# Key pages into the recurrent branch, later stores, a shorter weight lead: one edit to the order of work in a decoder layer

## The chip, the cores and the metric

The kernel runs on one core of a Trainium2 chip. The core has a matrix engine (TensorE, PE in the profile, with its weight loads as PEld), a vector engine (VectorE, DVE), an activation engine (ScalarE, ACT), a general engine (GpSimd, POOL) and a sync engine (SyncE, SP). In this kernel nearly every transfer between device memory and the on-chip buffer is issued from SP, in one order; sixteen DMA engines carry them out. Each engine runs its instructions in the order in which they were placed, and waits at an instruction until its operands and its buffer are there. The metric is the device time of one execution in microseconds (us), as the median of a few runs.

## The reference: one layer of a hybrid decoder

A prompt of 512 tokens and 8 sample sequences of one token each go through one layer with the same weights; the kernel treats them as 520 columns. Model width is 1024, there are 16 heads of 64.

```python
sh1, sc1, g1, sh2, sc2, g2 = ada_modulation(c, ada_w, ada_b)
h = rms_norm(x, norm1_g) * (1 + sc1) + sh1
xr, gr, q, k, v, fl, ga, gb = split(h @ w_in)
# branch A: recurrent
xc = causal_conv4(xr);  hr = rg_lru(xc)          # gates, exp, linear scan over time
ya = (hr * gelu(gr)) @ w_proj_a
# branch B: attention with a forget gate
logf = log_sigmoid(fl + b_f);  F = cumsum(logf)
s = q.k / 8 + F[t] - F[s]                         # prompt: causal, 512 x 512 per head
yb = (softmax(s) @ v) @ w_proj_b                  # samples: 1024 cached tokens and their own
# merge and feed-forward
x = x + g1 * ((sigmoid(ga) * ya + sigmoid(gb) * yb) @ w_o)
x = x + g2 * swiglu(rms_norm(x) * (1 + sc2) + sh2)
```

The samples' cached keys and values lie in pages of 128 tokens (128 x 1024 floats, 512 KB). Each of the 8 sequences has 8 key pages and 8 value pages, found through a page table. Outputs are the layer's result, k, v and logf of all tokens, and the states of the convolution and of the recurrence.

## The kernel before: units of work, and page work hung between them

**Units.** All large products are cut into units of 128 output columns: a product of the 1024 x 128 weight tile with the 1024 x 520 activations. For precision both are split into a high and a low part, so that a unit is 48 matmuls in two halves of 260 columns (`half_product`, line 231). The units have one fixed order. Units 0 and 1 are the last two of q; 2 to 31 are the recurrent branch (xr, gr, ga, gb of eight tiles i, in four stages of two tiles; the first stage is units 2 to 7, the others have eight each); 32 to 41 are k of tile 0, the eight units of the projection `pa`, and v of tile 0; 42 to 55 are k and v of tiles 1 to 7 inside the attention loop; 56 and 57 are the last two gb units; then come `pb`, `w_o` and the feed-forward part.

**Weights ahead.** `begin` opens a unit. It issues the loads of later weights (`load_chunks`, two buffers `wraw` of 1 MB) up to a reach of 22 us of estimated unit time, and splits weights (`split_upto`: ACT makes `whi`, DVE makes `wlo`, lines 197 and 198; three buffers each) up to a reach of 11 us. One unit counts 0.67 x 8 = 5.4 us in that estimate, so the reaches are four units and two units.

**Pages between units.** The samples' attention over the cache is done in small steps between units:

- `key_page` loads a key page (line 587) into one of seven buffers `pg` and multiplies it on POOL with the sequence's query `qb` (line 603); `qb` takes one of the seven buffers for eight pages.
- `key_sums` then reduces the page on DVE (line 614), a number of ticks after the load. 16 key pages (two sequences) make one group r.
- `past_softmax` is the softmax chain of a group, in five steps over successive ticks (lines 640 to 670), across DVE, PE, ACT and DMA.
- `sample_values` multiplies a pair of value pages with the weights of a group (line 687, matmuls on PE). Eight pairs make a group; `value_pages` keeps one pair loaded ahead.

`tick(keys, values)` does these in the order sums, chain steps, value pairs, key pages. It is called from `begin` for units 4 to 41, where the tables `KEYS` and `VALUES` tell how many key pages and whether a value pair; and from `at(i, part)` four times in each iteration i of the attention loop, by `KEYS_AT` and `VALUES_AT`. In `begin` the key pages come last, behind the weight loads. A step can only be taken when the one before it has been: a value pair of a group is skipped while the group's chain isn't done.

**The recurrent branch.** Per tile: convolution (`conv`, DVE lines 798 and 800, with the gate weights `gws`), two gate products (`lru_gates`), exponentials on ACT and line 829 on DVE (`lru_exp`), the scan over time on DVE (`lru_scan`, lines 840 to 843), and the product with the gelu (`lru_mul`, `lru_g`).

**The forget chain.** `log_forget` (lines 545 to 561) loads the logits, forms log sigmoid on ACT and DVE in small instructions, stores it, loads it back as 16 rows, fills a tile `fone` of ones on POOL (line 559), scans with it on DVE (line 560) and stores the sums `ftd` (line 561). It is called in the first stage, behind the second convolution.

**The attention loop.** Iteration i has the unit of k of tile i+1 and of v of tile i+1 (in the last iteration the two gb units), and around them for tile i: the transposes of v (`v_tokens`), the transposes of the probabilities (`turn`), scores and softmax of the next tile (`scores`), and the product with the values (`values`). `q_load` and `decay_rows` load q and the forget sums `fb` of a tile; `fm` (line 999) is made of `fb` on POOL.

**Stores.** `gate_b`, `branch_a`, `k_product` and `v_product` each end with a store of their result (lines 870, 879, 952, 975), issued right behind the unit.

**Who sets the order.** A list scheduler places the instructions of each engine when the kernel is built. It follows the order of the text as a priority and puts an instruction later where it takes its operands to be late. `issue_after` pins an instruction behind another on its engine; a key sum is pinned behind the last split (`state["last"]`).

## Time and profile before

| what | us |
|---|---|
| median of 3 runs | 1132.02 |
| lowest and highest of them | 1130.69, 1138.16 |
| the profiled execution's own time | 1130.33 |
| its span, first to last instruction | 1128.6 |
| PE busy in the span | 1052.2 |
| DVE, ACT, POOL busy | 654.1, 496.8, 295.7 |
| data moved | 206.95 MB |

All durations come from the one profiled execution. Its own time is 1.7 us above its span, and 1.7 us below the median of the runs. A busy time is the union of an engine's instructions; a busy PE isn't always a PE at full rate, since its clock can be granted below full speed (row `PEclk`, in tenths) and a matmul that waits inside its queue counts as busy.

Along the span, by the profile: norm, first modulation and q up to about 105 us; the recurrent branch from there to 313; `pa` to 381; the attention loop from 381 to 625; `pb` and `w_o` to about 725; the feed-forward part to the end.

### The profile page before, as it was taken

Reading aid. Unit: us, or ns where it says so; the run is one execution under the profiler, and the core shown is the slowest. Engines: PE = TensorE matmul, PEld = TensorE weight load, DVE = VectorE, ACT = ScalarE, POOL = GpSimd, SP = SyncE. Lnnn points to the kernel's source line nnn. Section 1 sums busy time; section 2 is a strip of 40 time slices with the busy share of each in tenths; the row PEclk is TensorE's granted clock in tenths of the full one; section 3 lists DMA queues with packets and bytes.
Section 4 is the critical chain, followed back from the end, with each engine's and each line's share of the span. In section 5 each row is a group of like instructions: output and inputs, shape, how many; then the busy total and the mean of one; then the engine's idle time right before and its main releaser. Section 6 shows DMA issues by size and latency. Waiting matters only on the chain.

```text
span 1128.6 us, 21038 instructions
## 1 busy us (share of the span) xinstructions
PE 1052.2 (93%) x8210; PEld 959.4 (85%) x8210; DVE 654.1 (58%) x1265; ACT 496.8 (44%) x983; POOL 295.7 (26%) x262
## 2 busy tenths in 40 slices
PE   4999969999998988878899899999999999999996
PEld 2877969999987856656678798999999999999995
DVE  6445897777775767967665454763334333443355
ACT  4424545777722555545567223453321233212352
POOL 2202571214244667757330001410000000000013
PEclk9999989999999998889899899999999999999998
DMA  9795655566689799998886485222323333242312
GB/s 336 266 346 175 211 189 163 177 209 172 212 287 295 192 318 300 292 284 291 246 229 241 150 292 179 75 76 76 113 75 105 83 89 99 79 109 76 94 57 76
DMA packets 164982, 206.95 MB, mean 183 GB/s; under 512 B 9475, under 2 KB 125715, under 8 KB 164819
## 3 DMA queue, kind: packets, MB, share of 16 engines
q1 hardware_dynamic: 164802, 205.09, 57.4%
q8 instruction: 64, 1.05, 0.4%
q0 software_dynamic: 80, 0.52, 0.2%
q14 instruction: 36, 0.29, 0.1%
HBM read 192.49 MB, written 13.09 MB: 182 GB/s over the span
## 4 chain that ended last, share of the span: by engine, by line
PE 67%; DVE 9%; DMA 5%; ACT 3%; issue 1%; POOL 1%; SPq 0%; DVEq 0%; POOLq 0%; ACTq 0%
PE fo L231 11%; PE fiu L231 10%; PE fig L231 10%; PE pb L231 4%; PE pa L231 4%; PE v L231 3%; PE pv L687 3%; PE ga L231 3%; PE wo L231 2%; PE k L231 2%; PE gb L231 2%; PE gr L231 2%; DVE wlo L198 2%; PE po L1073 1%; DMA pg<-in_cache_v_dram 1%
## 5 line engine op out<-in xcount | busy, mean ns | idle before, releaser
L198 DVE TENSOR_TENSOR wlo<-wraw,whi 128x1024 fp32r<-128x1024 f32 (+1 forms) x131 | 166.2, 1269 | 151.9 <-ACT whi L197 151.6
L197 ACT CAST whi<-wraw 128x1024 fp32r<-128x1024 f32 (+1 forms) x131 | 136.5, 1042 | 224.2 <-PE fo L231 74.6
L603 POOL TENSOR_TENSOR pg<-pg,qb 128x1024 f32<-128x1024 f32 x64 | 164.9, 2589 | 131.6 <-DMA pg<-in_cache_k_dram 109.3
L306 POOL TENSOR_TENSOR ss<-ss,sq 128x260 f32<-128x260 f32 x18 | 13.6, 755 | 424.8 <-ACT sq L305 424.4
L614 DVE TENSOR_REDUCE S<-pg 128x16 f32<-128x1024 f32 x64 | 77.1, 1211 | 40.2 <-POOL pg L603 40.2
L231 PE MATMUL fiu<-h2h,whi 128*128 128x260 f32 x320 | 90.5, 283 | 0.0
L231 PE MATMUL fig<-h2h,whi 128*128 128x260 f32 x320 | 90.4, 283 | 0.0
L231 PE MATMUL fiu<-h2l,whi 128*128 128x260 f32 x320 | 90.4, 283 | 0.0
L231 PE MATMUL fig<-h2l,whi 128*128 128x260 f32 x320 | 90.4, 283 | 0.0
L231 PE MATMUL fiu<-h2h,wlo 128*128 128x260 f32 x320 | 90.3, 282 | 0.0
L231 PE MATMUL fig<-h2h,wlo 128*128 128x260 f32 x320 | 90.3, 282 | 0.0
L231 PE MATMUL fo<-ach,whi 128*128 128x260 f32 x292 | 82.6, 283 | 0.0
L231 PE MATMUL fo<-acl,whi 128*128 128x260 f32 x292 | 82.5, 283 | 0.0
L231 PE MATMUL fo<-ach,wlo 128*128 128x260 f32 x292 | 82.5, 283 | 0.0
L687 PE MATMUL pv<-pg,pw 128*32 128x512 f32 x256 | 53.3, 668 | 15.6 <-DMA pg<-in_cache_v_dram 11.4
L231 PEld LDWEIGHTS fiu<-h2h,whi 128*128 128x128 f32 x320 | 60.2, 188 | 0.0
L231 PEld LDWEIGHTS fig<-h2h,whi 128*128 128x128 f32 x320 | 60.2, 188 | 0.0
L231 PEld LDWEIGHTS fig<-h2h,wlo 128*128 128x128 f32 x320 | 60.2, 188 | 0.0
L231 PEld LDWEIGHTS fiu<-h2h,wlo 128*128 128x128 f32 x320 | 60.2, 188 | 0.0
L231 PEld LDWEIGHTS fiu<-h2l,whi 128*128 128x128 f32 x320 | 60.2, 188 | 0.0
L231 PEld LDWEIGHTS fig<-h2l,whi 128*128 128x128 f32 x320 | 60.2, 188 | 0.0
L1024 ACT ACTIVATE p<-p,mu 128x128 f32<-128x128 f32 (+3 forms) x64 | 35.5, 556 | 47.7 <-DVE mu L1022 47.5
(373 smaller groups left out, 3452.6 us busy)
## 6 DMA issues: line engine op xcount, KB each, us to landing
pg<-in_cache_k_dram SPq DMA_DIRECT2D x64, 512.0 KB, 5.8
pg<-in_cache_v_dram SPq DMA_DIRECT2D x64, 512.0 KB, 6.2
araw<-in_ada_w_dram SPq DMA_DIRECT2D x48, 512.0 KB, 7.4
wraw<-in_w_fi_dram SPq DMA_DIRECT2D x44, 512.0 KB, 5.2
wraw<-in_w_in_dram SPq DMA_DIRECT2D x34, 512.0 KB, 6.2
wraw<-in_w_in_dram SPq DMA_DIRECT2D x11, 1024.0 KB, 5.7
wraw<-in_w_fo_dram SPq DMA_DIRECT2D x8, 1024.0 KB, 5.2
x<-in_xT_dram SPq DMA_DIRECT2D x16, 260.0 KB, 6.1
```

Source lines behind the costliest of these rows:

```text
L197: state["act"] = act.copy(hi[:, :k1 - k0], src)
L198: state["last"] = dve.tensor_tensor(lo[:, :k1 - k0], src, hi[:, :k1 - k0].bitcast(F32), ALU.subtract)
L231: pe.matmul(out[:, :HALF], lhsT=wt[k], rhs=at, start=k == 0 and m == 0, stop=k == nk - 1 and m == 2)
L306: eng.tensor_tensor(acc[:, t0:t1], acc[:, t0:t1], q_, ALU.add)
L603: pool.tensor_tensor(pg, pg, qb[0], ALU.mult)
L614: dve.tensor_reduce(S[r // 2][:, c:c + H], pg.rearrange("p (h d) -> p h d", d=DH), AX.X, ALU.add)
L687: pe.matmul(pv[0][32 * gq:32 * gq + 32, :], lhsT=pw[r][:, c:c + 32], rhs=pgs[gq // 2][:, 512 * hf:512 * hf + 512], start=j == 0, stop=j == ...
L1024: act.activation(p[:, :n + 128], p[:, :n + 128], AF.Exp, bias=mu[:, 1:2], scale=-1.0, accum_out=mu[:, 2:3])
L1073: pe.matmul(po[:, 128 * kb:], lhsT=kvs[i]["v"][kb // 2][:, kb % 2, 128 * a:128 * a + 128], rhs=pair[m][:, o_:o_ + n], start=kb == 0 and m ...
```

## The change: where pages, stores, splits and the forget chain are put

The page work, the arithmetic and the units stay the same. What is moved:

- **Key pages.** `KEYS` now gives 48 pages to units 4 to 41 where it gave 38: 36 to units 4 to 31 (24 before) and 12 to units 32 to 41 (14 before). `KEYS_AT` gives 16 to the attention loop (26 before), one per part in iterations 0 to 3; before it was six in each of these and two in iteration 4. In `begin` the key pages now come ahead of the weight loads and of the sums, and in `tick` behind the load of a value pair.
- **Value pairs.** `VALUES` has 11 units from 21 on (8 before, from 26 on). `VALUES_AT` has three and two pairs in turn, where it had three in each iteration.
- **Stores.** Four kinds of stores (sB, tA, kT, vT) are put into a list and issued by `flush`, at the end of the next `begin` or `at`.
- **Weights in attention.** The reaches are set to 14 us (two units) for loads and 8 us (one unit) for splits from the start of the attention loop until the end of iteration 6, and back to 22 and 11 then.
- **Forget chain.** `log_forget` is called at the end of the second stage, not in the first. Its scan multiplies with a broadcast of a column of ones in place of the tile `fone`, so the fill on POOL goes.

```diff
-    state = {"n": 0, "dma": 0, "split": 0}
+    state = {"n": 0, "dma": 0, "split": 0, "load": 22, "lead": 11}
+    stores = []
+
+    def store(dst, src):
+        stores.append((dst, src))
+
+    def flush():
+        while stores:
+            sp.dma_start(*stores.pop(0))
+
-    KEYS = {4: 2, 5: 2, 6: 2, 7: 2, 12: 2, 13: 1, 14: 2, 15: 1, 20: 2, 21: 1, 22: 2, 23: 1, 28: 1, 29: 1, 30: 1, 31: 1,
-            32: 1, 33: 2, 34: 1, 35: 2, 36: 1, 37: 2, 38: 1, 39: 2, 40: 1, 41: 1}
-    VALUES = range(26, 42, 2)
+    KEYS = dict(zip(range(4, 42), (2, 2, 2, 2, 0, 1, 0, 1, 2, 2, 2, 2, 0, 1, 0, 1, 2, 2, 2, 2, 0, 1, 0, 1, 1, 2, 1, 2,
+                                   1, 1, 1, 1, 2, 1, 1, 2, 1, 1)))
+    VALUES = range(21, 42, 2)
...
-        load_chunks(units[reach(n, last, 22)][0])
-        split_upto(reach(n, last, 11))
-        if 4 <= n < 42:
-            tick(KEYS.get(n, 0), n in VALUES)
+        paced = 4 <= n < 42
+        if paced:
+            key_pages(KEYS[n])
+        load_chunks(units[reach(n, last, state["load"])][0])
+        split_upto(reach(n, last, state["lead"]))
+        if paced:
+            tick(0, n in VALUES)
+        flush()
...
-        fone = slot("fone", NP, parts=H)
-        pool.memset(fone, 1.0)
-        dve.tensor_tensor_scan(fcs, fone, lf[:, :NP], 0.0, ALU.mult, ALU.add)
+        dve.tensor_tensor_scan(fcs, one_col[:H].to_broadcast([H, NP]), lf[:, :NP], 0.0, ALU.mult, ALU.add)
...
+    def key_pages(n):
+        for _ in range(n):
+            if keys_todo:
+                key_page(*keys_todo.pop(0))
...
         some_values(values)
-        for _ in range(keys):
-            if keys_todo:
-                key_page(*keys_todo.pop(0))
         value_pages()
+        key_pages(keys)
...
-        sp.dma_start(sBd[i], t)
+        store(sBd[i], t)
...
-        sp.dma_start(tAd[i], tA[i])
+        store(tAd[i], tA[i])
...
-            log_forget()
...
             both(lru_exp, i)
+            if i == 2:
+                log_forget()
...
-        sp.dma_start(kT[128 * i:128 * i + 128, :], t)
+        store(kT[128 * i:128 * i + 128, :], t)
...
-        sp.dma_start(vT[128 * i:128 * i + 128, :], t)
+        store(vT[128 * i:128 * i + 128, :], t)
...
-    KEYS_AT = [(2, 1, 2, 1)] * 4 + [(2, 0, 0, 0)] + [(0, 0, 0, 0)] * 3
-    VALUES_AT = [(1, 1, 0, 1)] * 7 + [(1, 2, 1, 0)]
+    KEYS_AT = [(1, 1, 1, 1)] * 4 + [(0, 0, 0, 0)] * 4
+    state.update(load=14, lead=8)
+    VALUES_AT = [(1, 1, 0, 1), (1, 0, 0, 1)] * 3 + [(1, 1, 0, 1), (1, 1, 1, 1)]
 
     def at(i, part):
         tick(KEYS_AT[i][part], VALUES_AT[i][part], 2)
+        flush()
...
         if i == KT - 2:
             merge_load(0)
+            state.update(load=22, lead=11)
 
     def join():
+        assert not values_todo and not chains
```

## The prediction, made before the result was known

> **What bounds the kernel now.** I read the page's first two parts, then cut the attention loop and the branch into stretches, then read who waits for whom, last the instructions in order of time.
>
> ```profile
> span 1128.6 us, 21038 instructions
> PE 1052.2 (93%) x8210; PEld 959.4 (85%) x8210; DVE 654.1 (58%) x1265; ACT 496.8 (44%) x983; POOL 295.7 (26%) x262
> ...
> PEclk9999989999999998889899899999999999999998
> DMA  9795655566689799998886485222323333242312
> ```
>
> PE is busy for 93% of the span, so only its 76 us of idle time and its slowed clock can be won. The DMA row has a plateau of 8 and 9 in slices 14 to 21, and 5 and 6 in slices 4 to 10: the engines that bring pages are full in attention and half empty in the branch. The next view gives busy time per engine for the attention loop's first seven of eight iterations (cut where the k unit starts) and for `pa`; the last three columns are the granted clock, the DMA share and the rate.
>
> ```profile
> 381.20:414.90 33.70, 27.45 (x182) 20.91 (x182) 22.96 (x53) 16.67 (x42) 22.49 (x12) 0.95 0.89 253
> 414.90:446.60 31.70, 27.49 (x177) 20.94 (x176) 23.93 (x63) 18.75 (x47) 27.01 (x19) 0.89 0.91 302
> 446.60:479.40 32.80, 29.17 (x183) 22.74 (x182) 30.46 (x75) 18.27 (x48) 24.12 (x17) 0.90 0.97 292
> 479.40:513.90 34.50, 27.81 (x178) 21.09 (x179) 21.96 (x59) 18.17 (x47) 22.35 (x16) 0.90 0.86 258
> 513.90:544.80 30.90, 27.11 (x177) 21.27 (x177) 22.01 (x65) 17.33 (x45) 18.12 (x13) 0.89 0.92 302
> 544.80:576.30 31.50, 26.78 (x185) 20.86 (x183) 20.32 (x65) 19.11 (x50) 9.62 (x11) 0.95 0.85 226
> 576.30:601.60 25.30, 25.30 (x188) 19.93 (x189) 14.86 (x53) 18.18 (x47) 7.47 (x7) 1.00 0.88 307
> ...
> 313.00:381.20 68.20, 62.92 (x465) 55.38 (x466) 44.14 (x82) 19.45 (x38) 31.27 (x18) 0.97 0.89 289
> ```
>
> Iteration 6 is the yardstick: PE busy throughout, at full clock, 25.3 us. Iterations 0 to 4, in which key pages run, take 163.6 us together, 32.7 each, at clocks of 0.89 to 0.95 and a DMA share of 0.86 to 0.97. Iteration 5 has no key page and still takes 31.5. The waits of the attention loop (total us, times, longest):
>
> ```profile
> PE pv L687 <- DMA pg<-in_cache_v_dram: 11.4, 7, 3.7
> PE pv L687 <- ACT pw L658: 4.1, 1, 4.1
> ...
> SPq L975 <- ACT vt L250: 29.5, 6, 6.8
> SPq L870 <- ACT sB L869: 10.5, 1, 10.5
> SPq L879 <- DVE tA L878: 7.8, 1, 7.8
> SPq L952 <- ACT kt L944: 4.2, 4, 3.0
> ```
>
> PE's largest wait is for value pages. SP stands 52.0 us at the four kinds of stores, because each is issued before its result exists, and every page load behind it stands too.
>
> In the recurrent branch, by stage:
>
> ```profile
> 120.60:170.20 49.60, 39.83 (x316) 39.23 (x316) 48.38 (x35) 24.18 (x41) 34.49 (x16) 0.90 0.55 187
> 170.20:217.90 47.70, 47.36 (x396) 47.15 (x394) 33.99 (x45) 31.90 (x58) 11.00 (x8) 1.00 0.54 172
> 217.90:262.00 44.10, 44.10 (x362) 43.51 (x363) 33.48 (x48) 33.70 (x58) 7.89 (x7) 1.00 0.55 173
> 262.00:313.00 51.00, 50.87 (x416) 46.75 (x415) 38.86 (x49) 36.48 (x65) 20.07 (x7) 1.00 0.65 202
> ```
>
> PE is the bound in the last three; in the first, DVE is busy 98% and PE idles 9.8 us. Why DVE is full there:
>
> ```profile
> PE gr L231 <- DVE wlo L198: 8.0, 2, 7.7
> ...
> 120.65 8.11 DVE L560 TENSOR_TENSOR_SCAN fcs<-fone,lf 16x512 f32<-16x512 f32 x1 [4.24 <-POOL fone L559]
> ...
> 158.47 2.31 DVE L800 SCALAR_TENSOR_TENSOR xc<-prm,xc 128x8 f32<-128x8 f32 x1
> 166.87 0.21 DVE L800 SCALAR_TENSOR_TENSOR xc<-prm,xc 128x8 f32<-128x8 f32 x1
> ...
> 120.10 0.52 POOL L559 MEMSET fone<- 16x512 f32 x1
> 120.58 7.10 POOL L603 TENSOR_TENSOR pg<-pg,qb 128x1024 f32<-128x1024 f32 x3
> ...
> SPq L561 <- DVE fcs L560: 14.6, 1, 14.6
> SPq L587 <- DVE S L614: 16.4, 10, 5.2
> ```
>
> The scan of the forget chain first waits 4.24 us for the fill with ones on POOL, then takes 8.11 us beside three page products. It isn't alone: the same 128x8 instruction takes 0.21 us or 2.31 us, the long one beside page products. SP stands 14.6 us at the store of the scan's result, with pages and weights behind it.
>
> **The change, part by part.**
>
> *Pages leave attention.* DMA time in iterations 0 to 4 is share times length: 30.0 + 28.8 + 31.8 + 29.7 + 28.4 = 148.7 us. Rate times length gives 45.9 MB, so 3.24 us per MB, and 1.70 us for a page of 512 KB. Ten key pages go, one of the three query broadcasts (same size), and two value pairs of 15 (3+2+3+2+3 remain), four pages: 15 x 1.70 = 25.5 us. Left are 123.2 us, 24.6 per iteration, just under PE's 25.3. Today an iteration loses (163.6 - 148.7) / 5 = 3.0 us beyond its DMA time. I take the larger limit plus that loss, 28.3: 5 x 28.3 = 141.5, **-22.1 us**. Iteration 5 holds the 4.1 us wait for the last group's softmax; that group's pages now end an iteration earlier, so 28.3 here too, **-3.2 us**. The last two iterations stay. Ends: all six at 25.3, 195.1 - 151.8, gives -43.3; all of 0 to 4 at iteration 5's 31.5 gives -6.1.
>
> Those ten pages also leave POOL and DVE in attention; neither is the bound in iteration 6, so I count nothing for it.
>
> *Stores later.* No instruction is added. The 52.0 us that SP stands go, and value pages start sooner; that is how the 28.3 is reached, so it isn't added again. Each store still has its room behind it. Their tiles live a unit longer in the 60 slots of the heap; I see no row that prices it and count nothing between 0 and one store's wait, 6.8 us.
>
> *Weights less far ahead.* Same loads and splits, later. A unit lasts about 12.6 us in attention (half of 25.3). The row below lands a load in 6.2 us, and the split behind it takes 1.28, so one unit of lead covers both. I take nothing; if the queue delays a load by a whole unit, 6.2 us once per tile is the end, and that is part of the 3.0 kept.
>
> ```profile
> wraw<-in_w_in_dram SPq DMA_DIRECT2D x34, 512.0 KB, 6.2
> ...
> L198 DVE TENSOR_TENSOR wlo<-wraw,whi 128x1024 fp32r<-128x1024 f32 x22 | 28.2, 1280 | 13.8 <-ACT whi L197 13.6
> L614 DVE TENSOR_REDUCE S<-pg 128x16 f32<-128x1024 f32 x15 | 18.0, 1209 | 0.0
> ...
> L829 DVE SCALAR_TENSOR_TENSOR th<-gate,th 128x520 f32<-128x520 f32 x8 | 12.8, 1602 | 5.0 <-ACT gate L828 5.0
> L800 DVE SCALAR_TENSOR_TENSOR xc<-prm,xc 128x8 f32<-128x8 f32 x21 | 10.9, 517 | 0.0
> L842 DVE TENSOR_TENSOR gate<-a,prm 128x8 f32<-128x8 f32 x8 | 6.8, 849 | 8.7 <-ACT a L826 8.7
> ...
> 255.42 0.17 DVE L842 TENSOR_TENSOR gate<-a,prm 128x8 f32<-128x8 f32 x1 [4.20 <-ACT a L826]
> 258.65 0.69 DVE L829 SCALAR_TENSOR_TENSOR th<-gate,th 128x520 f32<-128x520 f32 x1
> ...
> L603 POOL TENSOR_TENSOR pg<-pg,qb 128x1024 f32<-128x1024 f32 x25 | 69.7, 2803 | 94.6 <-DMA pg<-in_cache_k_dram 84.3 <-DMA gw<-in_gates_dram 7.5 <-PE gate L817 2.8
> ```
>
> *Forget chain.* In the built order of the changed kernel the small steps of log sigmoid stay in the first stage; the scan and its store move into the second. The first stage loses 4.24 us of waiting and the scan's 8.11, more than PE's 9.8 us of idle time: **-9 us** (ends 0 and -9.8). The scan with the broadcast operand has no row; it costs between 1.2 us (a scan of that length elsewhere in the branch) and 8.11. I take 4, as page products will run beside it again.
>
> *Pages enter the branch.* Units 8 to 31 get 28 key pages, where 16 were. Each costs a reduction of 1.21 us on DVE, and holds other DVE instructions while its product runs. The hold per page is between 0 and 2.1 (2.31 less 0.21). Three groups show it in the branch: 8 x (1.60 - 0.69) + 21 x (0.52 - 0.21) + 8 x (0.85 - 0.17) = 19.2 us over 25 pages, 0.8 each; with the groups not quoted I take 1.0. So 12 x 2.2 = 26.5 us. The second group's softmax chain moves here from `pa`: I estimate 5 us for its six DVE steps, the longest of which took 2.17 us for the first group. DVE in the last three stages goes from 106.3 to 106.3 + 26.5 + 4 + 5 = 141.8 of 142.8 us: full. The first stage shows what a full DVE costs, 9.8 us in 50. The splits' lead of two units (11.5 us) delays that, and the load isn't even, so I take one such loss and less, **+8 us**, with ends 0 and 3 x 9.8 = 29.4.
>
> ```profile
> 241.33 2.17 DVE L649 TENSOR_SCALAR dg<-cs,st 32x256 f32<-32x256 f32 x1
> ```
>
> *`pa`.* Two key pages fewer, value pairs equal: 3.4 us less DMA time where PE idles 5.3 us: **-1 us**.
>
> The GPSIMD Engine Reference of the Trainium skill (section "8. Key points") says that GpSimd and VectorE contend for SBUF when the vector instruction has two SBUF inputs or a two-port mode. The trace agrees for the 128x8 instruction (2.31 against 0.21 us) and hardly for the two-input split, whose mean is 1.28 against 1.21 for a reduction with one input. What it would make of the time if all of it held is the second rival.
>
> Sum: -22.1 - 3.2 - 9 + 8 - 1 = -27.3 us, from the profiled execution's 1130.3 to **1103 us**. That execution is 1.7 us below the median of the runs.
>
> **The rivals.**
>
> *Attention isn't bound by DMA.* Iteration 5 speaks for it: 31.5 us with no key page at 226 GB/s, so the chain of splits, scores and transposes across engines may set the pace. Iteration 6, with more bytes per us (307) and no loss, speaks against. Then iterations 0 to 4 give only 6.1 us, and with -2 for the rest: 1122 us.
>
> *Every page holds DVE for its whole product.* Twelve more products of 2.37 us (7.10 for three) hold 28.4 us in place of the 12 counted: DVE is over its room in the branch by the 16 us of difference and PE waits for it: 1103 + 16 = 1119 us. For it: the first stage. Against: the groups above, which show 0.8 us a page. This is the rule quoted above, taken at full strength.
>
> *Slower: pages ahead of weights choke SP.* In `begin` the page loads now stand ahead of the weight load. A page load waits for one of seven buffers, which a reduction on a full DVE frees; behind it stand the weights, the gate weights and the stores, and behind these ACT's and DVE's splits and PE. The longest such wait today is 5.2 us. I count twelve units of stages two to four, the ones that take two pages or load weights behind one; from 27.3 / 12 = 2.3 us lost at each the kernel is slower. At two thirds of 5.2 us, 3.5 each, 42 us are lost: 1103 + 42 = 1145 us. Against it: the reach of four units is 23 us, and a load lands in 6.2.
>
> *The change doesn't do what it says*: value pairs are skipped because a group's chain is late, and pages fall back into attention. The tables give 16 pages by unit 14 and the first pair at unit 21, seven ticks later for five steps, so this is unlikely: 1130 us.
>
> *More than forecast*: iterations at 25.3 and no loss in the branch, -43.3 - 9 = -52: 1078 us.
>
> **How the numbers follow.** Forecast 0.52, attention bound elsewhere 0.12, full hold 0.11, choked queue 0.12, no effect 0.05, more than forecast 0.08. About 1% is what a measurement here can tell from no change: 1119 to 1141 counts as same when put against 1130.3. Faster gets the forecast, the better case, and something under half of the two rivals at 1122 and 1119: 0.69. Same gets the rest of these and no effect: 0.19. Slower is the choked queue: 0.12. The range leaves out most of the better case and the choked queue, and reaches from 1086 to 1130.
>
> **What would show it.** Right: iterations 0 to 4 near 28 us with a PE clock above 0.95 and a DMA share still above 0.9; PE's wait for value pages under 6 us; SP's wait at the four stores gone; no PE idle time of 8 us in the first stage; DVE above 0.9 in stages two to four with few PE gaps. Wrong: iterations still at 31 us with a falling DMA share (bound elsewhere); PE waits for `wlo` in stages two to four above 15 us in all (hold); SP waiting for pages with weights landing late (choke).

## The result, and the profile after

| | before | changed |
|---|---|---|
| median, us | 1132.04 | 1119.75 |
| lowest to highest, 4 runs each | 1130.69 to 1138.16 | 1117.42 to 1121.52 |
| span of the profiled execution | 1128.6 | 1117.0 |

The ratio is 0.988, with a 95% interval of 0.9839 to 0.9921: the kernel is faster by 12.3 us, where 27.3 were forecast. First the page of the changed kernel: span, busy time, granted clock and DMA share in 40 slices.

```profile
span 1117.0 us, 21038 instructions
...
PE 1046.2 (94%) x8210; PEld 960.8 (86%) x8210; DVE 660.9 (59%) x1265; ACT 496.2 (44%) x982; POOL 297.8 (27%) x261
...
PEclk9999989999899989898999999999999999999998
DMA  9795857577779777787985595123324242332312
```

The DMA row is more even now: mostly 5 to 8 where the branch had 5 and 6, and the plateau of 8 and 9 in attention has broken up. So pages did move. The eight iterations of the attention loop of the changed kernel, cut as before (busy time of PE, PEld, DVE, ACT, POOL, then clock, DMA share and rate):

```profile
386.20:424.60 38.40, 30.31 (x183) 22.57 (x182) 23.47 (x51) 13.78 (x34) 15.31 (x12) 0.87 0.59 192
424.60:459.20 34.60, 26.92 (x171) 22.13 (x170) 21.73 (x60) 18.60 (x47) 21.15 (x14) 0.85 0.77 226
459.20:487.00 27.80, 26.25 (x180) 20.14 (x179) 21.27 (x58) 17.99 (x46) 17.58 (x12) 1.00 0.83 278
487.00:518.90 31.90, 25.95 (x169) 22.47 (x168) 24.05 (x65) 18.22 (x46) 22.11 (x14) 0.84 0.76 242
518.90:542.80 23.90, 23.90 (x181) 19.71 (x179) 20.59 (x62) 18.69 (x46) 9.36 (x10) 1.00 0.92 262
542.80:573.00 30.20, 27.46 (x198) 20.80 (x198) 16.97 (x64) 18.33 (x48) 9.01 (x10) 1.00 0.90 275
573.00:595.10 22.10, 22.10 (x177) 19.57 (x176) 15.73 (x54) 18.30 (x48) 7.42 (x7) 1.00 0.90 335
595.10:615.20 20.10, 18.53 (x155) 17.38 (x153) 13.59 (x48) 17.41 (x35) 1.31 (x1) 1.00 0.36 126
```

Iterations 2 and 4 are what was forecast or better. Iterations 0, 1 and 3 are not, and their DMA share is 0.59 to 0.77: it isn't mainly pages that they lack. In each of the three PE is idle for 6 to 8 us **and** runs at a clock of 0.84 to 0.87. The branch of the changed kernel, by stages, the last cut at the beginning of `pa` (in the kernel before, `pa` begins at 310.3 us, 2.7 us ahead of the cut at 313):

```profile
120.60:170.20 49.60, 44.11 (x351) 43.90 (x350) 44.47 (x45) 27.64 (x50) 38.87 (x18) 0.93 0.60 204
170.20:217.90 47.70, 45.93 (x377) 45.07 (x377) 43.51 (x48) 31.13 (x54) 21.83 (x11) 1.00 0.65 195
217.90:262.00 44.10, 44.10 (x363) 41.17 (x363) 34.13 (x40) 26.38 (x48) 19.90 (x9) 1.00 0.83 270
262.00:322.00 60.00, 53.76 (x414) 49.18 (x413) 49.02 (x60) 39.20 (x66) 26.23 (x15) 0.94 0.73 230
```

The second and third stage take their pages nearly without loss, and DVE is far from full in the third. The fourth loses. To see what was lost as what, I split each stretch three ways: PE's idle time; the loss to the clock (busy time times one less the granted clock, summed over stretches of 2 us); and the rest, which is PE's own work. The difference of after to before, in us (the first two rows are the branch, with the first stage's forecast in the first and that of the pages in the second):

| stretch (us, before / after) | all | idle | clock | own work | forecast |
|---|---|---|---|---|---|
| 105 to the end of the last xr unit (269 in both) | 0 | -2.8 | +0.7 | +2.2 | -9 |
| from there to k of tile 0 (35.4 / 45.8) | +10.4 | +6.2 | +3.0 | +1.1 | +8 |
| k of tile 0 and `pa` (76.6 / 71.4) | -5.2 | -3.6 | 0 | -1.6 | -1 |
| attention (243.6 / 229.0) | -14.6 | -5.1 | -2.6 | -6.8 | -25.3 |
| `pb` to the end (504.0 / 501.8) | -2.2 | +0.1 | -3.0 | +0.7 | 0 |

The sum is the 11.6 us of the span. Within attention, iterations 0 to 4 fell by 7.0 (22.1 forecast), iteration 5 by 1.3 (3.2), and 6 and 7 by 6.1 (none forecast). The own work of -6.8 there is mostly value pairs: 24 fewer of their matmuls (three pairs), which keep PE busy for 31.7 us where it was 41.9 (slowed clock included), and 24 in the last two iterations where 48 were. Some of them appear as the +2.2 in the branch.

### Where the fourth stage lost: a small instruction beside a page product

The fourth stage of the changed kernel in stretches of 4 us (same columns), where before PE was busy throughout:

```profile
276.00:280.00 4.00, 4.00 (x36) 4.00 (x36) 2.99 (x7) 2.19 (x5) 0.40 (x3) 1.00 1.05 394
280.00:284.00 4.00, 1.96 (x17) 1.75 (x15) 4.00 (x4) 0.00 (x0) 4.00 (x2) 1.00 0.15 58
284.00:288.00 4.00, 0.74 (x3) 0.74 (x4) 4.00 (x4) 1.70 (x5) 2.19 (x1) 0.81 0.71 187
288.00:292.00 4.00, 4.00 (x21) 4.00 (x20) 4.00 (x5) 3.72 (x7) 0.49 (x1) 0.50 0.99 339
292.00:296.00 4.00, 4.00 (x28) 3.02 (x28) 3.29 (x4) 3.69 (x9) 1.90 (x1) 0.83 0.48 160
```

ACT does nothing from 280 to 284 and PE next to nothing from 282 to 288; then PE runs at half clock for 4 us. The instructions of POOL, DVE and ACT there, in order of time (start, duration, then who ended the idle time):

```profile
279.71 0.22 DVE L814 SCALAR_TENSOR_TENSOR xc<-prm,xc 128x8 f32<-128x8 f32 x1
...
279.92 6.26 POOL L614 TENSOR_TENSOR pg<-pg,qb 128x1024 f32<-128x1024 f32 x2 [2.00 <-DVE xc L814]
...
280.51 2.34 DVE L814 SCALAR_TENSOR_TENSOR xc<-prm,xc 128x8 f32<-128x8 f32 x1
...
283.91 2.30 DVE L814 SCALAR_TENSOR_TENSOR xc<-prm,xc 128x8 f32<-128x8 f32 x1
...
286.30 0.62 ACT L270 CAST xch<-xc 128x520 fp32r<-128x520 f32 x1 [7.03 <-DVE xc L814]
286.83 0.38 ACT L871 ACTIVATE ge<-gr 128x260 f32<-128x260 f32 x1
```

Two page products run from 279.92 us on; both are done after 6.26 us. The 128x8 instruction ahead of them takes 0.22 us, the two beside them 2.34 and 2.30. ACT stands 7.03 us at `xch`, which needs the last of them; behind it on ACT stands `ge`, which empties the buffer that PE's next product needs. The view of PE's waits of this stage has it:

```profile
PE ga L244 <- ACT ge L871: 5.3, 1, 5.3
```

That the products are the cause is shown by the runs without them, below. The clock adds to it: behind 5.3 us of idle time in two stretches PE got half its clock. The Trainium skill has this as a rule (TensorE: Matmul & The Clock Gate, section "Part 1: The HAM clock gate (the "warmup" mystery)"): an idle window of some 3.4 us halves the clock, and a busy one of that length restores it. The trace agrees: 0.50 from 288 to 292 us, behind the gap, and 0.83 in the next stretch, in which the full clock comes back. So 6.2 us of idle time in this stage cost 9.2.

### Where attention lost: the third group's chain at the seam

The changed kernel around the end of `pa` (386.1) in stretches of 4 us: PE busy, clock, DMA share, rate.

```profile
384.00:388.00 4.00, 4.00 (x35) 1.00 0.05 18
388.00:392.00 4.00, 2.72 (x19) 1.00 0.17 67
392.00:396.00 4.00, 1.06 (x8) 0.97 0.00 0
396.00:400.00 4.00, 4.00 (x17) 0.61 0.98 98
400.00:404.00 4.00, 2.25 (x19) 1.00 0.67 258
404.00:408.00 4.00, 1.88 (x8) 0.75 1.02 416
408.00:412.00 4.00, 4.00 (x15) 0.50 1.04 379
```

From 384 to 396 next to no byte moves, PE idles, and then the clock falls. On PE the instruction that stands is the first matmul of the softmax chain of the third group of pages (`lgt`); it waits for `mk` on DVE, which is made of the reductions just ahead of it. DVE and PE in order of time:

```profile
387.26 1.22 DVE L625 TENSOR_REDUCE S<-pg 128x16 f32<-128x1024 f32 x1 [2.68 <-POOL pg L614]
...
392.25 1.21 DVE L625 TENSOR_REDUCE S<-pg 128x16 f32<-128x1024 f32 x1
393.49 0.68 DVE L654 TENSOR_TENSOR S<-S,suf 128x128 f32<-128x128 f32 x2
394.21 0.59 DVE L656 TENSOR_REDUCE mk<-S 128x32 f32<-128x256 f32 x1
...
394.94 0.27 PE L659 MATMUL lgt<-cs,mk 128*32 128x128 f32 x1 [4.22 <-DVE mk L656]
```

In the kernel before, the third group's chain came in iteration 2: `lgt` ran at 457.0, and PE waited 0.8 us for it. Inside `pa` it was the second group's, at 356.4. PE's wait for both in the kernel before (in all, times, longest; the longest is that in `pa`):

```profile
PE lgt L645 <- DVE mk L642: 4.8, 2, 4.0
```

So the price of a chain that comes due while its sums are late, some 4 us of PE, was there to read before the change. In the changed kernel the second group's `lgt` runs at 301.3, in the fourth stage, without a wait, and the third group's has taken the place at the seam.

DMA stood still because SP stood, at the store of `tA` from 380.0 for 8.8 us and at that of `st` from 389.2 for 6.3. SP's waits from 386 to 596 in the changed kernel: the three of the four kinds of stores that fall there (issued from one line now) and the `st` of the chain:

```profile
SPq L168 <- ACT vt L263: 31.2, 6, 8.7
SPq L168 <- ACT kt L959: 20.3, 5, 6.3
SPq L168 <- DVE tA L892: 8.8, 1, 8.8
...
SPq L665 <- DVE st L661: 6.3, 1, 6.3
```

The first three are 60.3 us up to the end of iteration 6; before, the same three were 41.5 us there (29.5, 4.2 and 7.8). The rest of the prediction's 52.0 is 10.5 at an sB store, which lies in the last iteration and stays, with 8.3. Moving the stores in the text did not free SP. PE's waits for value pages did fall, from 11.4 us to the first row below, which is of the whole span:

```profile
PE pv L701 <- DMA pg<-in_cache_v_dram: 4.0, 3, 1.8
PE v L244 <- DVE pl L1059: 5.2, 2, 2.6
PE sc L1031 <- DVE v L1003: 4.6, 2, 2.6
```

The other two rows are of the iterations 1 and 3, one wait of each kind in either. There PE stands behind DVE's work for the attention products (`pl` and `v` are the low parts of the probabilities and of v), not behind a chain of pages. These are the two long iterations to which the tables give two value pairs and not three. No run here takes these waits away, so what sets them stays open.

### The profile page after: what moved, and what is told of

It reads as the page before. It is cut to its first block, busy times and chain, and to the rows that moved or that the text cites. A ratio compares the mean times of both kernels' runs of the same rounds, so it can differ in the third digit from the quotient of the medians.

```text
span 1117.0 us, 21038 instructions
## 1 busy us (share of the span) xinstructions
PE 1046.2 (94%) x8210; PEld 960.8 (86%) x8210; DVE 660.9 (59%) x1265; ACT 496.2 (44%) x982; POOL 297.8 (27%) x261
## 4 chain that ended last, share of the span: by engine, by line
PE 72%; DVE 12%; DMA 7%; ACT 3%; issue 3%; POOL 2%; SPq 1%; DVEq 0%; POOLq 0%; ACTq 0%
PE fo L244 11%; PE fig L244 10%; PE fiu L244 10%; PE pb L244 4%; PE pa L244 4%; PE v L244 3%; PE ga L244 3%; PE wo L244 3%; DMA pg<-in_cache_k_dram 2%; DVE wlo L207 2%; PE pv L701 2%; PE k L244 2%; PE xr L244 2%; PE qp L449 2%; PE gb L244 2%
## 5 line engine op out<-in xcount | busy, mean ns | idle before, releaser
L207 DVE TENSOR_TENSOR wlo<-wraw,whi 128x1024 fp32r<-128x1024 f32 (+1 forms) x131 | 171.1, 1307 | 151.1 <-ACT whi L206 150.4
L244 PEld LDWEIGHTS fig<-h2l,whi 128*128 128x128 f32 x320 | 60.3, 188 | 0.0
L244 PEld LDWEIGHTS fo<-ach,wlo 128*128 128x128 f32 x292 | 55.0, 188 | 0.0
L244 PEld LDWEIGHTS fo<-acl,whi 128*128 128x128 f32 x292 | 55.0, 188 | 0.0
```

The source lines that it names most:

```text
L207: state["last"] = dve.tensor_tensor(lo[:, :k1 - k0], src, hi[:, :k1 - k0].bitcast(F32), ALU.subtract)
L244: pe.matmul(out[:, :HALF], lhsT=wt[k], rhs=at, start=k == 0 and m == 0, stop=k == nk - 1 and m == 2)
```

## The experiments

Times are medians, each beside runs of the kernel before on the same chip; the ratio to it stands with its 95% interval.

### Each part alone, on the kernel before

**Pages alone**: the tables and the place of the key pages in `begin`, as in the change.

```diff
-    VALUES = range(26, 42, 2)
+    KEYS = dict(zip(range(4, 42), (2, 2, 2, 2, 0, 1, 0, 1, 2, 2, 2, 2, 0, 1, 0, 1, 2, 2, 2, 2, 0, 1, 0, 1, 1, 2, 1, 2,
+                                   1, 1, 1, 1, 2, 1, 1, 2, 1, 1)))
+    VALUES = range(21, 42, 2)
...
+        if paced:
+            key_pages(KEYS[n])
...
+    KEYS_AT = [(1, 1, 1, 1)] * 4 + [(0, 0, 0, 0)] * 4
+    VALUES_AT = [(1, 1, 0, 1), (1, 0, 0, 1)] * 3 + [(1, 1, 0, 1), (1, 1, 1, 1)]
```

> The kernel before with the page part alone (the new tables of key pages and value pairs, and key pages ahead of the weight loads). Theory 1 (the pages are the whole gain; the other parts matter little): 1116 to 1122 us, as the full change, with the fourth stage of the branch again about 11 us longer than before and attention about 14 us shorter. Theory 2 (the pages alone lose in the branch what they win in attention, and the forget chain is what pays): 1128 to 1134 us.

Measured 1126.76 us, 0.9958 [0.9936, 0.998]. Attention falls from 243.6 to 232.9 us, and k of tile 0 starts at 319.0 us where it was 304.4. PE has the same 5.3 us wait of `ga` for `ge` in the fourth stage, and iteration 0 takes 38.5 us. Both losses belong to the pages. The time lies between the two ranges expected: the gain in attention came, and the branch took more of it back than in the change.

**Stores alone**: only the list and `flush`.

```diff
+        flush()
...
-        sp.dma_start(vT[128 * i:128 * i + 128, :], t)
+        store(vT[128 * i:128 * i + 128, :], t)
```

> The kernel before with the later stores alone. Theory 1 (the scheduler puts a store back to where it takes its data to be ready, so SP stands at it as long as before, about 50 us in attention): within 4 us of before. Theory as predicted (SP is freed for pages): 1120 us or less, with SP's waits at the four stores in attention under 15 us.

Measured 1144.93 us, 1.0116 [1.0082, 1.0151]: slower. Attention takes 258.4 us. The view of PE's waits there, for this run:

```profile
PE v L241 <- DVE pl L1054: 22.2, 5, 8.4
```

This wait was 3.4 us before. With the old page places, stores put later cost some 13 us by the ratio, and PE loses the most behind `pl` on DVE. Neither theory held, and no run tells why `pl` came so late.

**Shorter weight lead alone**, and **forget chain alone**:

```diff
+    state.update(load=14, lead=8)
...
+            state.update(load=22, lead=11)
```

> The kernel before with the shorter weight lead in attention alone. Theory 1: no cost, no gain, within 4 us of before. Theory 2 (fewer splits ahead of the scores free DVE and ACT at the right moment, or SP is freed from standing at a weight buffer): 1122 to 1128 us.

```diff
-        dve.tensor_tensor_scan(fcs, fone, lf[:, :NP], 0.0, ALU.mult, ALU.add)
+        dve.tensor_tensor_scan(fcs, one_col[:H].to_broadcast([H, NP]), lf[:, :NP], 0.0, ALU.mult, ALU.add)
...
-            log_forget()
...
+            if i == 2:
+                log_forget()
```

> The kernel before with the forget chain moved and its fill gone, alone. Theory as predicted: the first stage loses its idle time of PE, 1121 to 1124 us. Theory 2 (the stall of the first stage comes from page products beside short vector instructions and stays; after has 5.5 us of it left): 1127 to 1132 us.

Measured 1131.25 us, 0.999 [0.9978, 1.0002], and 1131.28 us, 0.9988 [0.9971, 1.0004]: neither can be told from no change. With the forget chain moved, the last xr unit ends 4.7 us earlier (264.4 against 269.1), and PE still waits 5.7 us for `wlo` in the first stage; k of tile 0 starts 4.7 us earlier too (299.7 against 304.4), and the whole doesn't show it. The scan with the broadcast operand took 1.2 us in the changed kernel, with no page product beside it.

The four ratios multiply to 1.005, that of the change is 0.988: the parts don't add.

### The change without one part

The three edits put the old code back for one part each.

```diff
-        store(vT[128 * i:128 * i + 128, :], t)
+        sp.dma_start(vT[128 * i:128 * i + 128, :], t)
```

> The changed kernel with its stores back at once behind their units (all other parts kept). Theory 1 (later stores cost attention some 12 us, as they did alone): 1105 to 1111 us. Theory 2 (the cost of the later stores belongs to the old places of the pages; beside the new ones they help): 1121 to 1128 us, attention 233 us or more where the full change has 229.

```diff
-    state.update(load=14, lead=8)
```

> The changed kernel with the weights loaded and split as far ahead in attention as before. Theory 1 (the lead doesn't matter, as it didn't alone): 1117 to 1122 us. Theory 2 (with the new places of the pages a long lead makes SP stand at a weight buffer with pages behind it): 1124 us or more.

```diff
+        fone = slot("fone", NP, parts=H)
+        pool.memset(fone, 1.0)
...
-            if i == 2:
-                log_forget()
```

> The changed kernel with the forget chain at its old place and with its fill on POOL. Theory 1 (the parts add up; alone the move gave 1 to 2 us, 4.7 of them in the branch and some lost later): 1120 to 1124 us. Theory 2 (the new order ahead of units pays only with the scan out of the first stage): 1126 us or more.

Measured: old stores 1120.66 us, 0.9882 [0.986, 0.9905]; old long lead 1115.63 us, 0.9841 [0.982, 0.9862]; old forget chain 1123.81 us, 0.9913 [0.9891, 0.9935]. So beside the new page places the later stores are worth nothing either way, which lies between the two theories. The forget chain is worth about 4 us by the medians, and the shorter lead may cost 4 us, which neither theory had; both intervals overlap that of the change. In the trace of the run with the old forget chain k of tile 0 starts 4.4 us later than in the change (319.2 against 314.8). Iteration 0 stays at 37.9 to 38.2 us in all three: none of them causes the seam.

### Without the page products

The product of the key pages on POOL is taken out, from the changed kernel and from the one before.

```diff
-        pool.tensor_tensor(pg, pg, qb[0], ALU.mult)
```

> The changed kernel without the product of each key page with the query on POOL: the page is reduced as it was loaded, so the samples' attention is computed from other scores (all loads, reductions and softmax steps are kept). Theory 1 (in the branch, page products on POOL hold DVE's short instructions, and that made the fourth stage 11 us longer): from the start of k of tile 0, which lies at 314.8 us in the changed kernel and at 304.4 before, 10 us or more come back, and the 128x8 instruction of the convolution never takes over 0.5 us. Theory 2 (the fourth stage is longer through the reductions, the softmax chain and the ScalarE table loads that came with the pages): k of tile 0 starts at 310 us or later.

> The kernel before without the product of each key page with the query (reduced as loaded, other scores, all loads and steps kept): the control for the same cut in the changed kernel, where k of tile 0 started at 294.4 us. Theory 1 (the products, by holding VectorE and making it wait, are what made the branch longer with more pages in it): k of tile 0 starts at 293 to 297 us here too, so without products the pages enter the branch for nothing; attention is then some 10 to 20 us longer than the 223 us of the changed kernel without products. Theory 2 (the pages lengthen the branch by themselves): 290 us or less.

From one execution each: 1086.86 us (change) and 1117.04 us (before). In the branch of both PE has neither an idle stretch nor a slowed one, the fourth stage included, and k of tile 0 starts at 294.4 and 291.7 us: 2.7 us apart, PE's moved work, where with products it is 10.4. (The control was expected at 293 to 297 or at 290 or less, and lies between.) The 128x8 instruction from 110 to 315 us, in the changed kernel (its group: busy time and mean) and in the run without products (shortest, middle and longest of 21):

```profile
L814 DVE SCALAR_TENSOR_TENSOR xc<-prm,xc 128x8 f32<-128x8 f32 x21 | 15.2, 723 | 0.1
```

```profile
L813 DVE SCALAR_TENSOR_TENSOR xc<-prm,xc x21: 218/222/230, 112.6 to 264.2; 128x8 f32<-128x8 f32 x21
```

No instruction of this kind is long without a product beside it: five of these 21 in the changed kernel take 2.3 to 2.4 us, and each lies beside one whole product. The scheduler's order changes too when the product goes, so the totals are not a clean price of it. Even so: without products the change shortens the time by 30.2 us and attention by 28.7, and with them the profiled executions by 11.6 and attention by 14.6. The products may thus have a part in what attention lost as well; with one execution each, and another order, that isn't shown.

### Where the third group's chain runs

**Chain into `pa`**: the pages of units 32 to 41 earlier, so that the group is complete two units sooner.

```diff
-                                   1, 1, 1, 1, 2, 1, 1, 2, 1, 1)))
+                                   2, 1, 1, 1, 2, 1, 2, 2, 0, 0)))
```

> The changed kernel with the last two key pages before the attention loop taken two units earlier (units 32 to 41 get 2, 1, 1, 1, 2, 1, 2, 2, 0, 0; same sum). Theory 1 (the first iteration is 38 us because the softmax chain of the third group starts at its seam, and SP and TensorE stand at it): the first iteration falls to 34 us or less, the whole to 1114 to 1117 us. Theory 2 (the first iteration is long for the place of its splits and stores, the chain is just there): first iteration still 37 to 39 us, 1118 to 1122 us.

Measured 1129.68 us, 0.9971 [0.9955, 0.9988]. Iterations 0 and 1 fall to 29.5 and 30.6 us, and `pa` grows from 64.3 to 75.5. The cost travels with the chain: PE now stands 5.7 us at `lgt` inside `pa`. The first theory was right about the iteration and not about the time.

**The `st` store later**: the store at which SP stood 6.3 us goes to the chain's last step.

```diff
-        sp.dma_start(mtd[32 * r:32 * r + 32, 0:1], st)
...
+        sp.dma_start(mtd[32 * r:32 * r + 32, 0:1], st)
```

> The changed kernel with the 32 x 1 store of the softmax chain's maxima issued three steps later, with the chain's other store. Theory 1 (SP stands 6.3 us at this store in the first iteration with the first loads of value pages behind it, and that costs PE time): first two iterations 4 us or more shorter in sum, 1114 to 1117 us. Theory 2 (PE isn't waiting for those loads): within 2 us of the changed kernel.

Measured 1117.74 us, 0.9866 [0.9835, 0.9897], 2 us less by the medians and not told from the change. Iteration 0 stays at 38.3 us. PE stands 4.3 us at `lgt` and 4.3 at `lgm`, the chain's next matmul (4.2 and 2.1 in the change). SP's stand at this store was not the cause.

**Attention's products on DVE**, with the old lead:

```diff
+        if s < 6:
+            pool.tensor_tensor(pg, pg, qb[0], ALU.mult)
+        else:
+            with tc.issue_after(state["last"].ins):
+                dve.tensor_tensor(pg, pg, qb[0], ALU.mult)
```

> The changed kernel with the old long weight lead (which alone took it to 1115.6 us) and with the products of the 16 key pages of attention on VectorE instead of GpSimd. Theory 1 (in attention, too, page products on GpSimd cost through waits across engines: reductions and softmax steps stand behind them): 1109 to 1113 us. Theory 2 (VectorE has less room than the waits cost): 1116 us or more.

Measured 1131.0 us, 0.9965 [0.9945, 0.9985], 15 us worse than the same kernel with the products on POOL (1115.63). Taking the products away from POOL isn't a way out while DVE has to do them in order.

### The order of pages, sums and loads

**Sums a unit later**, so that DVE doesn't stand at a reduction whose product is late:

```diff
-            tick(0, n in VALUES)
+            tick(0, n in VALUES, 2)
```

> The changed kernel with the reductions of key pages a unit later between units 4 and 41 (one unit after the load, as before, not in the same opening of a unit). Theory 1 (VectorE stood 16.1 us in the branch at reductions whose product wasn't done, and that made the branch longer, beside the held instructions): that wait falls under 6 us, k of tile 0 starts at 308 us or earlier, the whole at 1112 to 1116 us. Theory 2 (the held instructions alone do it; the scheduler had placed the reductions anyway): k of tile 0 within 3 us of 314.8, the whole within 3 us of the changed kernel.

Measured 1125.67 us, 0.9944 [0.9926, 0.9963]. DVE's 16.1 us of standing at reductions in the branch are gone, and k of tile 0 starts at 329.2 us, 14 later than in the change: PE stands 10.0 us at `lgt` and 8.2 at `lgs`, since the chain's operands are later. My idea that DVE's standing costs the branch fell. Iteration 0 still takes 38.2 us: PE stands 0.8 us at `lgt` there and 5.9 at `lgm`.

**Key pages behind the weight loads everywhere**, as in the kernel before:

```diff
-        if paced:
-            key_pages(KEYS[n])
...
-            tick(0, n in VALUES)
+            tick(KEYS[n], n in VALUES)
```

> The changed kernel with the key pages of units 4 to 41 behind the weight loads and the reductions, as before, at the new numbers per unit. Theory 1 (the place ahead of the weights costs the branch, through SP and through reductions placed too early): k of tile 0 starts 4 us or more earlier, the whole at 1113 to 1117 us. Theory 2 (only the number of pages counts in the branch): k of tile 0 within 3 us of 314.8, the whole 1118 us or more.

Measured 1122.36 us, 0.9904 [0.9866, 0.9942]. k of tile 0 starts at 332.3 us (314.8 in the change), with 7.5 us each at `lgt` and `lgs`; iterations 0 and 1 fall to 32.0 and 30.0. But this edit moves two things: with the loads, the reductions come a unit later, and the run above has that alone, with the loads still ahead. It already starts k of tile 0 14.4 of the 17.5 us later. So it is the early reductions that help the branch; the loads' place against the weights is worth some 3 us there. At the seam the later reductions alone changed nothing, and both together do.

**Four pages of units 24 to 31 to iteration 4**:

```diff
-    KEYS = dict(zip(range(4, 42), (2, 2, 2, 2, 0, 1, 0, 1, 2, 2, 2, 2, 0, 1, 0, 1, 2, 2, 2, 2, 0, 1, 0, 1, 1, 2, 1, 2,
+    KEYS = dict(zip(range(4, 42), (2, 2, 2, 2, 0, 1, 0, 1, 2, 2, 2, 2, 0, 1, 0, 1, 2, 2, 2, 2, 0, 0, 0, 0, 1, 1, 1, 1,
...
-    KEYS_AT = [(1, 1, 1, 1)] * 4 + [(0, 0, 0, 0)] * 4
+    KEYS_AT = [(1, 1, 1, 1)] * 5 + [(0, 0, 0, 0)] * 3
```

> The changed kernel with four key pages of the fourth stage of the branch (units 24 to 31: 4 in place of 8) put into iteration 4 of the attention loop. Theory 1 (the fourth stage loses its 11 us through the page products and through the second group's softmax chain in it): k of tile 0 starts at 308 us or earlier, iteration 4 grows by 5 to 7 us, and the whole is within 3 us of the changed kernel or better. Theory 2 (the loss of that stage comes from earlier stages, DVE being behind): k of tile 0 at 312 us or later, the whole 1122 us or more.

Measured 1125.29 us, 0.9923 [0.9897, 0.9949]. The wait of `ga` shrinks to 1.8 us, but k of tile 0 starts at 320.2: a chain step, `lgt`, now waits 7.2 us behind `gate` on DVE. Fewer pages in the stage don't help if another in-order step lands badly.

**Long lead and the later `st` store together**, the two edits given above:

> The changed kernel with the old long weight lead and the store of the maxima three steps later. Theory 1 (the two gains of 4 and 2 us add): 1112 to 1115 us, below both kernels. Theory 2 (both free SP at the same place): 1115 to 1118 us.

Measured 1114.14 us, 0.9837 [0.9806, 0.9867], inside the first theory's range, but not told from the long lead alone (1115.63). Iteration 0 takes 39.2 us.

### The seam alone

```diff
-        if paced:
+        if paced and n < 32:
             key_pages(KEYS[n])
...
-            tick(0, n in VALUES)
+            tick(0 if n < 32 else KEYS[n], n in VALUES)
```

> The change with one edit: in units 32 to 41 (pa and its two neighbours) key pages come behind the weight loads again, as in the kernel before; in units 4 to 31 they stay ahead. Theory A: iteration 0's loss at the seam comes from the order in units 32 to 41 alone. Then k of tile 0 starts near 315 us as in the change, iterations 0 and 1 fall from 38.4 and 34.6 to about 32 and 30 us as they did with all pages behind the loads, and the time is 1107 to 1112 us. Theory B: the gain in those iterations came from the longer branch, which gave the last chain and its loads more time. Then iterations 0 and 1 stay at 36 us and more and the time is 1117 to 1122 us. Theory C: the order in units 32 to 41 only moves time from the attention loop into pa. Then pa takes 67 us or more in place of 64 and the time is 1116 to 1122 us.

Measured **1109.31 us** (1107.57 to 1112.62), 0.9807 [0.9771, 0.9843]; the interval meets that of the change only at its end (0.9839 and 0.9843). k of tile 0 starts at 316.0, iterations 0 and 1 take 33.0 and 30.2 us, and attention 221.1: theory A. Theory C falls, since k of tile 0 and `pa` take 69.2 us, less than the 71.4 of the change. The edit moves the loads behind the weights and, with their later reductions, the third group's chain: in the text `lgt` goes from the first to the third of the four ticks of iteration 0 (the run with sums a unit later has it in the second, and gained nothing there). Which of the two gives the gain isn't separated. The same seven stretches around the end of `pa` (385.1) in this run:

```profile
384.00:388.00 4.00, 4.00 (x35) 1.00 0.49 192
388.00:392.00 4.00, 4.00 (x29) 1.00 0.58 205
392.00:396.00 4.00, 4.00 (x30) 1.00 0.79 269
396.00:400.00 4.00, 3.34 (x25) 1.00 0.98 308
400.00:404.00 4.00, 3.56 (x22) 1.00 1.02 401
404.00:408.00 4.00, 1.08 (x10) 1.00 1.03 316
408.00:412.00 4.00, 3.42 (x19) 0.75 0.05 16
```

PE is busy where it idled, and up to 408 the clock stays. The last reduction of this group starts at 396.24, and `lgt` runs at 408.3, 23 us into the iteration: it finds `mk` (398.21) done, and the 3.2 us that PE stands ahead of it are for `pl`. Over all runs with the new page places and the products, the place of this one matmul, and PE's stand at it and at `lgm`, go with the length of iteration 0:

| `lgt` of the third group, us into iteration 0 | PE's stand at `lgt` and `lgm` in it, us | iteration 0, us | runs |
|---|---|---|---|
| 8.2 to 9.1 | 5.9 to 8.6 | 37.9 to 39.2 | change, pages alone, the three without one part, `st` later, products on DVE, sums later, lead and `st` |
| 22.1 to 23.1 | 2.3 to 3.2 | 32.0 to 33.0 | pages behind everywhere, seam, seam with lead and `st` |
| 49.8 (in iteration 1) | none | 30.5 | four pages moved |
| 17.6 ahead of it (in `pa`) | none (5.7 in `pa`) | 29.5, `pa` 11 longer | chain into `pa` |

Without products `lgt` comes 5.1 us in, PE stands 2.5 us at the two, and the iteration takes 34.0. So the length goes with PE's stand at the chain rather than with an early place by itself, as far as one execution tells.

The last run has the long lead and the later `st` store as well:

> The change with the old long lead of weights, the st store at the last chain step, and key pages behind the weight loads in units 32 to 41. Theory A: the seam's gain adds to that of the two other edits (1114.1 us): 1103 to 1108 us. Theory B or C: no gain from the third edit, 1112 to 1117 us.

Measured 1114.07 us, 0.9862 [0.9814, 0.9909]: the gains don't add. Iterations 0 and 1 take 32.3 and 33.0, but iteration 5 takes 36.0 where it was 30.4: PE waits 4.5 us for a value page there. What the lead is worth changes sign with the order around it, and no run here tells why that page came late.

## Why the prediction was wrong, by its own steps

*Pages leave attention, -22.1; measured -7.0.* This is the step that failed. The DMA time in it was worked out well: share times length gives 118.6 us for iterations 0 to 4, against the 123.2 left by the forecast, and iterations 2 and 4 took 27.8 and 23.9 against 28.3. The error was to give every iteration the larger of two throughput limits and the loss of 3.0 us of the iterations before, and to put at nothing what an in-order step holds on PE. The tables give 48 pages, three groups, up to unit 41, so that the third chain begins at the seam. I asked when the last group ends, and never what the third one's matmuls would wait for at the start of iteration 0: PE stands 6.3 us there, with the clock behind it. With only the order of units 32 to 41 changed attention falls by 22.5 us from before (25.3 forecast), and iterations 0 to 4 by 15.2. So the seam explains 8.2 of the 15.1 us that were missed. The other 6.9 lie mainly in iterations 1 and 3, 30.2 and 31.8 us in that run too, where PE waits for `pl` and `v`; their cause stays open.

That 15.1 is nearly the whole miss of the span (27.3 forecast, 11.6 measured) is luck. Up to k of tile 0 the forecast was -1 and the measure +10.4, a second miss of 11.4 us; `pa`, the last two iterations and the end gave 12.5 back that nobody had forecast.

*SP's 52.0 us freed, as the way to the 28.3.* Wrong: at the same stores up to iteration 6 SP stood 60.3 us where it had stood 41.5. Alone the edit costs 13 us, in the change nothing. The step read a wait as if the text's order set it.

*Iteration 5, -3.2; measured -1.3.* The wait of 4.1 us went down to 1.3, but 40 matmuls of value pairs run there, where 24 did. Nothing was left over from earlier: by the end of iteration 4 all 24 pairs of the tables had run, and the scheduler took three pairs more into iteration 5 and left none for the last. The sequel, iterations 6 and 7 shorter by 6.1, was not in the sum. I had costed the value pairs as DMA time alone; PE's own 6.8 us in attention was the missing term.

*Forget chain, -9; measured -4.4 to -4.7* at k of tile 0, as the run that puts it back and the run of it alone have it; by whole runs it isn't clear of the noise. Mis-sized: the scan and its wait were not the only thing ahead of `wlo`, PE still waits 5.5 us. The scan's 1.2 us (4 taken) was its lower end.

*Branch, +8; measured some +14.7.* With the pages alone k of tile 0 starts 14.6 us later; in the change it is 10.4 later with the forget chain's 4.4 already won. Some 2.7 of it is PE's moved work, which the sum didn't have; the other 12 lie inside the stated ends, and above the 8. The place didn't hold: I let DVE run full over three stages, and the largest part (9.2 us of idle time and clock) came in the fourth, most of it from one pair of 128x8 instructions on the way of xc to ACT to PE. A product's hold on such an instruction is 2.1 us, as priced from the first stage; the mean over the pages, 1.0, says nothing of where it hits.

*Weight lead, 0.* Not shown wrong or right: nothing alone, some 4 us in the change, and the other way beside the seam edit, where the `st` store was moved as well.

*`pa`, -1; measured -5.2*, 3.6 of it idle time: the second group's `lgt`, at which PE stood 4.0 us inside `pa`, now runs in the fourth stage. The prediction took PE's idle time in `pa` for a matter of DMA.

Of the rivals, *attention isn't bound by DMA* came nearest, in time (1122, with 6.1 us for iterations 0 to 4, where 7.0 were measured) and in sign: a falling DMA share in long iterations. Its mechanism, the chain of splits, scores and transposes across engines, fits the waits for `pl` and `v` in iterations 1 and 3, and not iteration 0, where the chain of the pages stood. *Every page holds DVE* was right about the fourth stage and not about the other two. *Choked SP* did not happen: from 110 to 325 us PE waits 7.4 us for `wlo`, 5.5 of them in the first stage, and with the loads behind the weights again the branch is longer, not shorter (k of tile 0 later by 17.5 us, 14.4 of which go with the later reductions).

## What to carry to other kernels

When work is moved between stages, list the in-order steps that come due at the seam and ask what each will stand behind there, before throughput is added up; here a chain whose first matmul came due 14 us later gave some 10 us of two iterations back. Look for the same step in the profile before: PE's 4.0 us at `lgt` in `pa` was its price. Price a gap in PE with its clock: 6.2 us of idle time cost 9.2. And read which small instruction lies on the way to PE before spreading a mean hold over many.

## What was not expected of the hardware

A 128x8 instruction of VectorE takes 0.22 us, and 2.3 us beside one whole page product of GpSimd (2.4 us); all 21 take 0.22 to 0.23 without products. The granted clock went to 0.50 after gaps of 4 to 6 us and came back within one or two stretches of 4 us, so that the clock took 14.5 us of attention before the change, 11.9 after it, and 8.0 in the best run.
